# Decode attention of a streaming encoder on one core: the value products as fp32 matmuls on four 32-column tiles, the score products queued together

## The chip, the cores and the metric

The kernel runs as one program on one core of a Trainium2 chip. The metric is the device time of one execution in microseconds (us). Three executions of the kernel before took 1247.17, 1244.36 and 1243.08 us; the median is 1244.36 us. The engines are named as in the profile: PE is the matrix engine (PEld its weight loads), DVE the vector engine, ACT the scalar engine, POOL the gpsimd engine, SP the engine that here only issues DMAs.

## The reference, cut to what matters

One step of an encoder with two layers for two groups of requests: a prompt of 1024 new rows, and 8 running streams ("sequences") of 16 new rows each, whose 1024 old rows of keys and values lie in a cache. Layer 0 holds differential attention with 4 heads beside a gated MLP, and layer 1 a convolution. All is fp32. The change is in the attention of the 8 sequences:

```python
# per sequence: 16 queries, 4 heads, 1024 cached rows and 16 new ones; two maps c = 0, 1 of 64 columns each
s = jnp.einsum('bqhcd,bkhcd->bhcqk', q, k).astype(jnp.float32) * (A_HALF_DIM ** -0.5)
s = s + bias                                   # by relative position
p = jax.nn.softmax(s, axis=-1)
w = p[:, :, 0] - lam * p[:, :, 1]              # differential weights
o = jnp.einsum('bhqk,bkhe->bqhe', w, v)        # values, 128 columns a head
o = _rmsnorm(o, subln_g) * (1.0 - LAMBDA_INIT_0)
out_a = o.reshape(bsz, t, A_WIDTH) * jax.nn.silu(g_a)
y = x + jnp.einsum('bte,ed->btd', jnp.concatenate([out_a, out_b], axis=-1), w_out)
```

## The kernel before

**Stages.** Up to about 480 us the kernel makes the input projection and the attention and MLP of the prompt (its last pieces run beside the start of the next stage). From about 490 to 770 us runs the decode stage, `phase_decode`, which is what the change touches. Behind it stands layer 1 in its convolution form, `phase_conv`, up to the end at 1242 us.

**The decode stage** does two kinds of work at once. One is the attention of the 8 sequences. The other is the output projection of layer 0, `main(t)`, for the nine 128-row tiles t of prompt and sequences: 48 matmuls of 512 columns each in fp32r (L155, tile `out`), with `prep(t)` ahead of it, which loads the tile's inputs (`raw<-s_oa`, `raw<-s_ob`, L829 and L830) and transposes them (L165). The loop at the end of `phase_decode` runs over the sequences b and issues for each: the scores of b, `prep(b-2)`, the keys of b+1 (two of four chunks), the values of b-1, `main(b-2)`, the other two chunks of keys, the weights of b. Pieces of the load and split of `w_out0` (`wl`) lie between them in the first rounds.

- `keys_part` loads a 512 KB chunk of the key cache on SP's queue (L696) into a tile `raw`, of which there are three, shared with the loads of `prep` and `w_out0`; PE transposes it (L416, tile `tr`), and ACT and DVE copy the result into the tile `KT`, or `KTx` for the last chunk, which also holds the new keys (L417).
- `dscores` multiplies keys by queries: for each of four parts of the keys, four matmuls, one a head, on four tiles of 32 columns of the array (L730). A bias, a row maximum (L735) and an exponential (L743) follow.
- `dweights` turns the exponentials into transposed, folded weights `wt` with 9 small matmuls (L758), and splits them into an fp32r high part (ACT, L761) and an fp32r rest (DVE, L762).
- `dvalues` loads four 512 KB chunks of the value cache on POOL's queue into two buffers `vraw` (L772), splits each into `vh` (ACT, L775) and `vl` (DVE, L776), and makes two matmuls of 512 columns in fp32r for each of 9 key tiles (L783, L784, and L786 for the new values `vs`). As every query row meets all four heads' columns, a mask keeps its own head (`om`, L788), an fp32 matmul puts the 16 rows in their place among 128 (L790), and DVE adds them to `oacc` (L794).
- `dfinish` normalises `oacc` once behind the last sequence, multiplies it by the gate and stores it to `s_oa`, from which `prep(8)` reads.

**What sets the order.** The code is handed to a scheduler that places each instruction on its engine by a simulated timeline, so that the order on an engine is not the order of the code. `tc.high_priority(offset=...)` moves what is issued under it ahead in this order. Each engine then runs its list strictly in order, and waits where a value isn't there yet. POOL and SP issue their DMAs from these lists too.

Of the kernel before, what the change touches and what calls it, by code (L numbers as in the profile page):

```python
# [19 lines left out]
P = 128  # L20
# [61 lines left out]
C_W = C_SAME + P  # L82
PE_TILES = (2, 4, 6)
# [19 lines left out]
class Builder:  # L103
# [544 lines left out]
    def decode_begin(self):  # L648
# [8 lines left out]
        vs = [ep.tile([P, 512], F32R, name=f"vs{i}", bufs=1) for i in range(2)]  # L657
        qs = [ep.tile([P, H, P], F32, name=f"qs{i}", bufs=1) for i in range(2)]
        oacc = ep.tile([P, 512], F32, name="oacc", bufs=1)
        mk = ep.tile([P, C_SGN - C_FOLD], F32, name="mk", bufs=1)  # L660
        fold, own, place = mk[:, :64], mk[:, 64:576], mk[:, 576:]
# [3 lines left out]
        def setup():  # L665
            nc.sync.dma_start(out=mk, in_=a["cst"][:, C_FOLD:C_SGN])
# [8 lines left out]
            nc.sync.dma_start(out=raw[:, 512:], in_=self.v0s)  # L675
            self.kt_copy(raw[:, :512], kTs, ptc, nc.scalar.copy)
            nc.scalar.copy(vs[0], raw[:, 512:])
            nc.vector.tensor_tensor(vs[1], raw[:, 512:], vs[0].bitcast(F32), ALU.subtract)
# [27 lines left out]
        self.dec = dec, ep, vp, ptc, vs, oacc, fold, own, place, bs0, seqs, keys_part, qz  # L706
        return [setup] + [lambda i=i: keys_part(0, (i,)) for i in range(4)]

    def phase_decode(self):
        nc, tc, a = self.nc, self.tc, self.a  # L710
        dec, ep, vp, ptc, vs, oacc, fold, own, place, bs0, seqs, keys_part, qz = self.dec
# [4 lines left out]
        pm = E(tc.tile_pool(name="pa", bufs=2, space=PSUM, reuse_waits="tile"))  # L716
# [3 lines left out]
        def dscores(b):  # L720
            q = qz[b % 2]
            S = []
            nm = self.small.tile([P, 4], F32, name="nm3")
            for i, parts in enumerate(((0, 1), (2,), (3,))):
                s = pS.tile([P, 512], F32, name="S")
                for j, p in enumerate(parts):
                    kt = seqs[b]["K"][p]
                    n = kt.shape[2]
                    for h in range(H):
                        nc.tensor.matmul(s[h * 32:(h + 1) * 32, j * n:(j + 1) * n], lhsT=q[:, h, :],  # L730
                                         rhs=kt[:, h, :], start=True, stop=True)
                S.append(s)
# [19 lines left out]
        def dweights(b):  # L752
            ex, cf = seqs[b]["ex"], seqs[b]["cf"]
            wt = ep.tile([P, 9, P], F32R, name="wt", bufs=1)
            for g0, g1 in ((0, 8), (8, 9)):
                ps = pm.tile([P, 512], F32, name="mm")
                for k in range(g0, g1):
                    nc.tensor.matmul(ps[:, (k - g0) * 64:(k - g0 + 1) * 64], lhsT=ex[:, k, :], rhs=cf,  # L758
                                     start=True, stop=True)
                pv = ps[:, :(g1 - g0) * 64].rearrange("p (k e) -> p k e", e=64)  # L760
# [452 lines left out]
```

## Time and profile before

| what | value |
|---|---|
| three executions | 1247.17, 1244.36, 1243.08 us |
| the profiled execution, its own time | 1244.07 us |
| its span in the trace | 1242.3 us |
| granted PE clock, mean | 0.975 of full |
| DVE busy | 807.9 us (65%) |
| ACT busy | 461.0 us (37%) |
| POOL busy | 364.3 us (29%) |

The span is what the trace covers; 1.8 us of the execution's own time lie around it. Times "at 652 us" below are counted from the start of the span. An fp32 matmul has two records in the trace, an fp32r matmul one. A record's duration overlaps the next one, so that what a matmul costs in a dense stretch is read from the distance of one start to the next.

### The profile page before, as it was taken

Reading aid. Unit: us, or ns where it says so; the run is one execution under the profiler, and the core shown is the slowest. Engines: PE = TensorE matmul, PEld = TensorE weight load, DVE = VectorE, ACT = ScalarE, POOL = GpSimd, SP = SyncE. Lnnn points to the kernel's source line nnn. Section 1 sums busy time; section 2 is a strip of 40 time slices with the busy share of each in tenths; the row PEclk is TensorE's granted clock in tenths of the full one; section 3 lists DMA queues with packets and bytes.
Section 4 is the critical chain, followed back from the end, with each engine's and each line's share of the span. In section 5 each row is a group of like instructions: output and inputs, shape, how many; then the busy total and the mean of one; then the engine's idle time right before and its main releaser. Section 6 shows DMA issues by size and latency. Waiting matters only on the chain.

```text
span 1242.3 us, 18215 instructions
## 1 busy us (share of the span) xinstructions
PE 1163.6 (94%) x6516; PEld 1038.4 (84%) x6516; DVE 807.9 (65%) x1663; ACT 461.0 (37%) x1058; POOL 364.3 (29%) x516
## 2 busy tenths in 40 slices
PE   6999999999989997779999998999999987998997
PEld 4878998999989987557776767999999987997886
DVE  5420225688787778765555444899989999267843
ACT  4431223545454545554435334111121212256421
POOL 2232223344354335322322220112424220033300
PEclk9999999999989998889999999999999998999999
DMA  8352444414141314877766646113321310212231
GB/s 298 107 157 73 148 145 136 126 55 120 41 122 46 103 49 137 287 246 238 238 220 237 194 145 174 45 41 89 97 85 60 112 60 24 68 35 102 80 124 68
DMA packets 122042, 153.23 MB, mean 123 GB/s; under 512 B 13697, under 2 KB 85401, under 8 KB 121944
## 3 DMA queue, kind: packets, MB, share of 16 engines
q1 hardware_dynamic: 107968, 108.21, 28.1%
q0 software_dynamic: 13840, 43.60, 10.5%
q8 instruction: 52, 0.85, 0.3%
q14 instruction: 38, 0.31, 0.1%
q10 hardware_dynamic: 144, 0.26, 0.1%
HBM read 116.22 MB, written 36.26 MB: 123 GB/s over the span
## 4 chain that ended last, share of the span: by engine, by line
PE 75%; DMA 9%; DVE 6%; issue 5%; ACT 3%; POOL 1%; SPq 0%; DVEq 0%; POOLq 0%; ACTq 0%
PE mm L155 51%; PE out L155 7%; PE py L1172 3%; PE pa L587 2%; PE tr L416 2%; DMA vraw<-in_cache_v 1%; PE tr L165 1%; PE S L544 1%; PE mm L784 1%; PE S L545 1%; PE mm L783 1%; PE tr L582 1%; DMA big<-s_c 1%; DMA s_c<-big 1%; PE S L730 1%
## 5 line engine op out<-in xcount | busy, mean ns | idle before, releaser
L155 PE MATMUL mm<-yh,wh 128*128 128x384 f32 x576 | 196.4, 341 | 15.2 <-ACT sg L1021 12.7
L155 PE MATMUL mm<-yh,wl 128*128 128x384 f32 x576 | 195.4, 340 | 0.2 <-DVE wl L144 0.2
L155 PE MATMUL mm<-yl,wh 128*128 128x384 f32 x576 | 195.4, 339 | 0.0
L155 PE MATMUL mm<-wh,xh 128*128 128x384 f32 (+1 forms) x504 | 185.4, 369 | 1.5 <-DVE sg L467 0.6
L1148 DVE SCALAR_TENSOR_TENSOR acc<-u,cc,acc 128x1024 f32<-128x1024 f32 x145 | 185.7, 1281 | 0.4
L155 PE MATMUL mm<-wl,xh 128*128 128x384 f32 (+1 forms) x504 | 184.3, 366 | 1.5 <-DVE wl L144 1.5
L155 PE MATMUL mm<-wh,xl 128*128 128x384 f32 (+1 forms) x504 | 183.5, 364 | 0.0
L144 DVE TENSOR_TENSOR wl<-raw,wh 128x1024 fp32r<-128x1024 f32 (+1 forms) x72 | 91.3, 1275 | 91.8 <-ACT wh L143 88.4
L155 PEld LDWEIGHTS mm<-yh,wh 128*128 128x128 f32 x576 | 109.2, 190 | 16.0 <-ACT sg L1021 13.0
L155 PEld LDWEIGHTS mm<-yh,wl 128*128 128x128 f32 x576 | 109.1, 190 | 0.6 <-DVE wl L144 0.5
L155 PEld LDWEIGHTS mm<-yl,wh 128*128 128x128 f32 x576 | 109.2, 190 | 0.3
L155 PEld LDWEIGHTS mm<-wh,xh 128*128 128x128 f32 x504 | 95.7, 190 | 13.1 <-issue 1.1
L155 PEld LDWEIGHTS mm<-wl,xh 128*128 128x128 f32 x504 | 95.6, 190 | 11.4 <-DVE wl L144 2.9
L155 PEld LDWEIGHTS mm<-wh,xl 128*128 128x128 f32 x504 | 95.5, 189 | 8.8 <-DVE xl L168 0.3
L143 ACT CAST wh<-raw 128x1024 fp32r<-128x1024 f32 (+1 forms) x72 | 71.4, 1001 | 70.0 <-PE mm L155 32.2
L124 POOL TENSOR_TENSOR rr<-pw,mhalf 128x1 f32<-128x1 f32 x59 | 38.4, 651 | 165.9 <-DVE pw L123 157.4
L558 ACT ACTIVATE e<-S,nm 128x512 f32<-128x512 f32 (+5 forms) x96 | 55.0, 578 | 53.7 <-DVE nm L553 36.2
L155 PE MATMUL out<-wh,ch 128*128 128x512 f32 x144 | 59.9, 416 | 1.7 <-DVE xr L844 1.2
L1166 POOL TENSOR_TENSOR tw<-wx,same 128x640 f32<-128x640 f32 x24 | 37.3, 1558 | 82.3 <-PE py L1172 72.5
L550 DVE TENSOR_REDUCE nm<-S 128x1 f32<-128x512 f32 (+5 forms) x96 | 52.5, 551 | 10.5 <-PE S L545 9.7
L155 PE MATMUL out<-wh,cl 128*128 128x512 f32 x144 | 58.8, 408 | 0.0
L155 PE MATMUL mm<-wl,ch 128*128 128x512 f32 x144 | 56.4, 392 | 2.3 <-DVE wl L144 2.2
(282 smaller groups left out, 2400.0 us busy)
## 6 DMA issues: line engine op xcount, KB each, us to landing
raw<-in_cache_k SPq DMA_DIRECT2D x32, 512.0 KB, 4.4
vraw<-in_cache_v POOLq DMA_DIRECT2D x32, 512.0 KB, 5.4
raw<-in_w_in SPq DMA_DIRECT2D x24, 512.0 KB, 5.1
raw<-in_w_out SPq DMA_DIRECT2D x16, 512.0 KB, 4.6
raw<-in_w_in SPq DMA_DIRECT2D x32, 256.0 KB, 3.4
raw<-in_w_in SPq DMA_DIRECT2D x48, 128.0 KB, 3.1
s_y<-xr POOLq DMA_DIRECT2D x9, 512.0 KB, 4.7
x<-s_y SPq DMA_DIRECT2D x9, 512.0 KB, 4.2
```

The lines of the kernel that those rows point to most:

```text
L124: m = nc.gpsimd.tensor_tensor(out, v[:, :w], self.mhalf[:, :w], ALU.pow)
L143: nc.scalar.copy(h[:, :ks * n], raw[:, :ks * n])
L144: (low or nc.vector).tensor_tensor(l[:, :ks * n], raw[:, :ks * n], h[:, :ks * n].bitcast(F32), ALU.subtract)
L155: m = self.nc.tensor.matmul(out, lhsT=x, rhs=y, start=(i == 0), stop=(i == n - 1))
L165: nc.tensor.transpose(ps[:, k * P:(k + 1) * P], src[:, kk * P:(kk + 1) * P], self.ident)
L416: nc.tensor.transpose(ps[:, h * P:(h + 1) * P], src[:, h * P:(h + 1) * P], self.ident)
L550: nc.vector.tensor_reduce(nm[:, j:j + 1], s[:, :n], AX.X, ALU.max, negate=True)
L558: nc.scalar.activation(e[:, j * n:(j + 1) * n], S[j][:, :n], AF.Exp, bias=nv, accum_out=zz[:, j:j + 1])
L587: nc.tensor.matmul(po, lhsT=wT[:, k * P:(k + 1) * P], rhs=hd["v"][:, k, :], start=(k == 0), stop=(k == qb))
L1148: tap = nc.vector.scalar_tensor_tensor(cv[:, :T] if k == CONV - 1 else acc, u[:, k:k + T], w1, acc, ALU.mult, ALU.add)
L1166: nc.gpsimd.tensor_tensor(tw.rearrange("p s (c f) -> p s c f", f=8), wx[:, g, :].rearrange("p (s f) -> p s f", f=8).unsqueeze(2).broadcast ...
L1172: nc.tensor.matmul(py, lhsT=tw[:, 4 - s, :], rhs=X[:, g, s:s + 176], start=(s == 0), stop=(s == 4))
```

## The change

The values stay fp32 and are not split. For each of the 9 key tiles, four matmuls of 128 columns, one a head, with the 16 query columns of that head's weights, write to four tiles of 32 columns of one PSUM bank, `pvt`. So each head's result lies apart: the mask, the placing matmul, `oacc` and `dfinish` go, and with them the split of the values and of the weights. Each sequence's result is squared and summed (ACT), scaled and gated by itself (DVE), with a gate `gs` that is loaded once at the start; the results of sequences 0 to 6 are stored by four DMAs, those of the last by four more. The values' load becomes `vload`, with eight buffers instead of two; the scores' 16 matmuls and the values' 36 are issued under `high_priority`. The scores' parts are taken in the order 3, 2, 0, 1, and the pool `pa` has one bank instead of two.

```diff
+HPS = 300
+VB = 8
...
-        oacc = ep.tile([P, 512], F32, name="oacc", bufs=1)
-        mk = ep.tile([P, C_SGN - C_FOLD], F32, name="mk", bufs=1)
+        fold = ep.tile([P, 64], F32, name="mk", bufs=1)
+        gs = ep.tile([P, NB, P], F32, name="gs", bufs=1)
+        og = ep.tile([P, NB, P], F32, name="og", bufs=1)
...
+            nc.gpsimd.memset(gs, 0.0)
+            for h in range(H):
+                nc.sync.dma_start(out=gs[h * 32:h * 32 + NQ], in_=self.s_ga[T:, h * P:(h + 1) * P].rearrange(
+                    "(b q) e -> q b e", q=NQ))
+            nc.sync.dma_start(out=vs, in_=self.v0s)
...
-            for i, parts in enumerate(((0, 1), (2,), (3,))):
+            S = [pS.tile([P, 512], F32, name="S") for _ in range(3)]
+            with tc.high_priority(offset=HPS):
+                for p, i, j in ((3, 2, 0), (2, 1, 0), (0, 0, 0), (1, 0, 1)):
...
+            wt = ep.tile([P, 9, 64], F32, name="wt", bufs=2)
...
+            nc.scalar.copy(wt[:, :8], ps.rearrange("p (k e) -> p k e", e=64))
+            nc.vector.tensor_copy(wt[:, 8], p8)
...
+        def vload(b):
+            if b >= NB:
+                return
+            cv = a["cache_v0"][b].rearrange("(t p) h e -> p t (h e)", p=P)
+            seqs[b]["V"] = []
+            for i in range(4):
+                vr = vp.tile([P, 1024], F32, name="vraw", bufs=VB).rearrange("p (t c) -> p t c", t=2)
+                nc.gpsimd.dma_start(out=vr, in_=cv[:, 2 * i:2 * i + 2])
+                seqs[b]["V"] += [vr[:, 0], vr[:, 1]]
+            seqs[b]["V"].append(vs)
...
         def dvalues(b):
-                    nc.scalar.copy(vh, vr)
-                    (nc.vector if i in VDVE else nc.gpsimd).tensor_tensor(vl, vr, vh.bitcast(F32), ALU.subtract)
...
-            nc.vector.tensor_tensor(om, pav, own, ALU.mult)
-            po = pm.tile([P, 512], F32, name="mm")
-            nc.tensor.matmul(po, lhsT=place[:, 112 - NQ * b:240 - NQ * b], rhs=om, start=True, stop=True)
...
+            pav = pvt[:, b % 2 * P:(b % 2 + 1) * P]
+            with tc.high_priority(offset=HPS):
+                for k in range(8, -1, -1):
+                    for h in range(H):
+                        nc.tensor.matmul(pav[h * 32:h * 32 + NQ], lhsT=wt[:, k, h * NQ:(h + 1) * NQ],
+                                         rhs=V[k][:, h * P:(h + 1) * P], start=(k == 8), stop=(k == 0))
...
+            nc.scalar.activation(jk, pav, AF.Square, accum_out=ss)
+            rm = self.small.tile([P, 1], F32, name="rr")
+            self.rpow(rm, ss, 1.0 / P, 1e-6)
+            nc.vector.scalar_tensor_tensor(og[:, b], pav, rm, gs[:, b], ALU.mult, ALU.mult)
...
         for b in range(NB):
             dscores(b)
...
             if b > 0:
                 dvalues(b - 1)
+                vload(b)
...
-        dfinish()
```

Three places show what the scheduler makes of it. The first is PE's list in a steady round, around the scores of a middle sequence (its queries are `qz_5777`; `tr` are transposes, of the keys under L416 and of `prep`'s input under L165). Before, word for word:

```order
L416 MATMUL tr<-cst_58,raw 128x128 x8
L758 MATMUL mm<-cf,ex 128x64 x9
L730 MATMUL S<-KT,qz_5777 32x256 x3
L416 MATMUL tr<-cst_58,raw 128x128 x4
L730 MATMUL S<-KT,qz_5777 32x256 x5
L165 MATMUL tr<-cst_58,raw 128x128 x4
L783 MATMUL mm<-vh,wt 128x512
L784 MATMUL mm<-vl,wt 64x512
```

Four pairs of value products (L783, L784) stand there in all, and then the last part of the scores, on `KTx`. In the changed kernel the same engine has, at the same place of a round (L736 are the scores, L786 the values, L418 and L167 the two kinds of transposes, L157 the output projection):

```order
L786 MATMUL pv<-vs,wt 16x128 x4
L786 MATMUL pv<-vraw,wt 16x128 x32
L157 MATMUL out<-wl,ch 128x512
L157 MATMUL out<-wh,cl 128x512
L157 MATMUL out<-wh,ch 128x512
L157 MATMUL out<-wl,ch 128x512
L157 MATMUL out<-wh,cl 128x512
L418 MATMUL tr<-cst_58,raw 128x128 x12
L167 MATMUL tr<-cst_58,raw 128x128 x4
L736 MATMUL S<-KTx,qz_5777 32x272 x4
L736 MATMUL S<-KT,qz_5777 32x256 x12
L167 MATMUL tr<-cst_58,raw 128x128 x4
```

The scores, which stood in three to four pieces between transposes and value products, are one piece of 16, and the values one of 36; the scores begin with the last chunk's part, right behind its transposes. Behind these rows stand 11 matmuls of the output projection before the next chunk of keys is transposed.

The second place is ACT's list between the last key copies of one round and the exponentials that follow (L743 before, L748 now). Before:

```order
L417 COPY KT<-tr 128x4x128
L173 ACTIVATE yn,ss<-xr 128x1024
L775 CAST vh<-vraw 128x1024
L177 ACTIVATE yn<-xr,rr 128x1024
L775 CAST vh<-vraw 128x1024
L417 COPY KTx<-tr 128x4x128
L167 CAST ch<-tr 128x512 x2
```

And now (L175 is the sum of squares over a finished tile of the output projection, L790 that over a sequence's values, L419 the key copies):

```order
L175 ACTIVATE yn,ss<-xr 128x1024
L419 COPY KT<-tr 128x4x128
L790 ACTIVATE jk,ss<-pv 128x128
L419 COPY KTx<-tr 128x4x128
L169 CAST ch<-tr 128x512
L179 ACTIVATE yn<-xr,rr 128x1024
L169 CAST ch<-tr 128x512
```

The casts of values are gone, a small sum of squares came in, and the copy into `KTx` stands behind both sums.

The third place is POOL's list where the decode stage starts (L772 and L776 load chunks of the value cache; L483, L469 and L485, L471 are MLP work of the prompt). Before:

```order
L738 MEMSET ex 128x128
L690 MEMSET qz_5778 128x128
L772 DMA vraw<-in_cache_v 128x2x512 x2
L483 TENSOR_TENSOR z_5513<-z_5510,lnb 128x128
L483 TENSOR_TENSOR z_5588<-z_5585,lnb 128x128
L469 TENSOR_TENSOR hh<-gl,sg 128x128
L772 DMA vraw<-in_cache_v 128x2x512
```

And now:

```order
L669 MEMSET gs 128x1024
L694 MEMSET qz_5777 128x128
L776 DMA vraw<-in_cache_v 128x2x512 x4
L743 MEMSET ex 128x128
L694 MEMSET qz_5778 128x128
L776 DMA vraw<-in_cache_v 128x2x512 x4
L485 TENSOR_TENSOR z_5513<-z_5510,lnb 128x128
```

Eight chunks, those of sequences 0 and 1, are issued where two were, ahead of the same MLP work, and a memset of the gate's tile stands in front.

81 lines of the change are left out of this document (22 added, 59 removed).

## The prediction

> **What bounds the kernel now.** I read the page first: the busy shares, the slices and the chain of work that ended last.
>
> ```profile
> span 1242.3 us, 18215 instructions
> PE 1163.6 (94%) x6516; PEld 1038.4 (84%) x6516; DVE 807.9 (65%) x1663; ACT 461.0 (37%) x1058; POOL 364.3 (29%) x516
> PE   6999999999989997779999998999999987998997
> PE 75%; DMA 9%; DVE 6%; issue 5%; ACT 3%; POOL 1%; SPq 0%; DVEq 0%; POOLq 0%; ACTq 0%
> ```
>
> PE is busy for 94% and carries 75% of the chain. The slices have one dip before the end, the 777 of the 16th to 18th slice, which is 466 to 559 us: the start of the decode stage. So the windows of that stage come next, cut at the start and then by rounds (PE's busy time is the second number, then the other engines, the granted clock, the DMA share and the rate):
>
> ```profile
> core 0: us, PE busy (x) PEld busy (x) DVE busy (x) ACT busy (x) POOL busy (x), PEclk, DMA share, GB/s
> 490.00:510.00 20.00, 14.07 (x95) 12.29 (x94) 16.30 (x48) 12.10 (x33) 9.00 (x20) 0.83 0.91 282
> 510.00:530.00 20.00, 11.23 (x107) 7.39 (x105) 11.04 (x24) 8.37 (x18) 4.57 (x10) 0.83 0.80 276
> 530.00:550.00 20.00, 16.27 (x98) 10.74 (x98) 15.61 (x23) 13.09 (x25) 4.68 (x6) 0.83 0.73 254
> 577.00:604.00 27.00, 27.00 (x165) 20.21 (x165) 15.77 (x29) 13.44 (x27) 11.20 (x13) 1.00 0.80 261
> 657.50:684.00 26.50, 26.03 (x159) 19.00 (x158) 15.32 (x26) 11.95 (x23) 6.99 (x10) 1.00 0.71 239
> 684.00:711.00 27.00, 24.45 (x118) 18.64 (x117) 13.87 (x22) 10.84 (x22) 5.81 (x8) 0.94 0.58 191
> ```
>
> The stage has two halves. From 490 to 550 PE idles for 5.9, 8.8 and 3.7 us, while the DMA share is 0.73 to 0.91. From 577 on a round takes 26.5 to 27 us and PE is full; ACT and DVE work about half of it. **What leaves PE in these rounds shortens them; what leaves DVE and ACT does not.** The chain of waits at the start says what the first half waits for:
>
> ```profile
> 504.68 4.76 DMA raw<-in_cache_k
> 516.81 6.55 DMA raw<-in_w_out
> 525.72 3.54 DMA raw<-in_w_out
> 544.02 6.51 DMA raw<-s_ob
> ```
>
> Loads of keys, of `w_out0` and of the first tile's inputs end the waits there.
>
> **The change part by part.** The rows of one round on PE:
>
> ```profile
> 651.40 1.03 PE L416 MATMUL tr<-cst,raw 128*128 128x128 f32 x8
> 652.36 0.64 PE L730 MATMUL S<-KT,qz 128*32 128x256 f32 x8
> 652.93 0.51 PE L783 MATMUL mm<-vh,wt 128*128 128x512 f32 x1
> 653.27 0.39 PE L784 MATMUL mm<-vl,wt 128*64 128x512 f32 x1
> 653.51 0.39 PE L783 MATMUL mm<-vh,wt 128*128 128x512 f32 x1
> ...
> 594.99 0.86 PE mm L790 x2
> ...
> 512.25 1.50 PE L730 MATMUL S<-KT,qz 128*32 128x256 f32 x24
> 513.57 0.64 PE L730 MATMUL S<-KTx,qz 128*32 128x272 f32 x8
> ```
>
> *Values (1).* Before, from start to start, a value product costs 0.24 us (653.27 to 653.51; I use 0.23 as the mean of such pairs), and a sequence has 18, so 4.1, and the placing matmul takes 0.86: 4.95 to 5.0 us. Afterwards there are 9 groups of four matmuls, 72 records. No row shows a 128-column matmul on a 32-column tile. The nearest is the scores: 24 records start within 1.32 us (512.25 to 513.57), so 0.055 a record and 0.44 for a group of 8 at 256 columns. One full-width record of 512 columns takes 0.43 (half of 0.86), so a record of 256 columns alone would take 0.215, and eight in 0.44 are four side by side with nothing left over. At 128 columns the group lies between 0.22, half of that, and 0.44, if a record costs 0.055 whatever its width. I take 0.30, nearer the lower end, since the scores' row shows no fixed cost above its streaming. Nine groups are 2.7; entering and leaving the tiled stretch I put at 0.3, of which more below. So 3.0 instead of 4.95 for each of six sequences (2 to 7): −1.95 × 6 = −11.7. The values of sequence 1 were multiplied beside the first full round; in the new order they stand ahead of the first output tile, where PE idles, so there the whole 4.95 leaves the full half. Sequence 0 was in the idle half before and stays. **Together −16.65.**
>
> The Trainium skill, page "TensorEngine Tiling (Array Packing)", section Instruction Overhead, speaks against taking so small a tile: each matmul has some 60 cycles of overhead on trn2, and the tiling factor should not be taken from a dimension that is already small. If that came on top of the streaming of 128 columns, a group would be near the upper bound and not at 0.30, and the time 1236.6 instead of 1229, which is the first rival below; the scores' row of this case shows no such addition at 256 columns, and no row shows 128.
>
> *Scores (2).* A group of eight records in a piece of its own takes 0.57 (652.36 to 652.93) instead of 0.44, and the rows beside such a piece stretch: 652.93 to 653.27 is 0.34 instead of 0.23. So a piece costs about 0.13 and some 0.1 to 0.2 beside it, 0.3 in all; this is also where the 0.3 of (1) is from. Three to four pieces become one: −0.75 us in each of five rounds (3 to 7). **−3.75.** That the values become one piece too is counted in (1).
>
> *Waits that go (3).*
>
> ```profile
> PE mm L784 <- DVE vl L776: 0.7, 3, 0.2
> 694.38 1.90 PE L758 MATMUL mm<-cf,ex 128*128 128x64 f32 x16
> 698.51 0.43 PE L758 MATMUL mm<-cf,ex 128*128 128x64 f32 x2 [2.24 <-DVE oacc L794]
> ```
>
> Value products waited 0.7 us in all for the rest `vl`, and the last weights 2.24 us for the bank that `oacc` freed late; behind this the clock in the window 684 to 711 is 0.94 instead of 1.00, 27 × 0.06 = 1.6 us of PE work. Neither `vl` nor `oacc` is left: **−4.** What is late next there is the exponentials of the last sequence, which no row shows to be late. The casts and subtractions of the values (ACT and DVE) go too, but those engines were not full: nothing.
>
> *Weights of sequence 2 (4).* They stood behind the first output tile, and stand ahead of it now, in the idle half. Nine of them cost 18 records at 0.117 (16 in 1.90): **−2.1.** The split of the weights goes, and stood beside other work: nothing.
>
> *Scores that wait for ACT (5), added.* The scores now begin with `KTx`, whose last copy stands on ACT behind two sums of squares.
>
> ```profile
> L844 DVE TENSOR_TENSOR xr<-xr,out 128x512 f32<-128x512 f32 x18 | 12.3, 683 | 29.4 <-PE out L155 29.4
> L173 ACT ACTIVATE yn<-xr 128x1024 f32<-128x1024 f32 x9 | 9.5, 1060 | 8.2 <-DVE xr L844 7.3 <-issue 0.9
> L800 ACT ACTIVATE jk<-oacc x4: 293/310/310, 723.7 to 725.9; 128x128 f32<-128x128 f32 x4
> L417 ACT COPY KTx<-tr x8: 565/577/585, 504.6 to 683.6; 128x512 f32<-128x512 f32 x8
> ```
>
> From the last output product on: DVE adds (0.68), ACT squares the tile (1.06, and 0.2 to read its sum out), squares the sequence's values (0.31, and 0.2), copies `KTx` (0.58): 3.0 us. PE meanwhile has 12 + 4 transposes, at 0.12 each (eight in 0.96, from 651.40 to 652.36): 1.9. So it waits 1.1, and I put 1.2 with the hand-over. Below, nothing, if the copy gets ready by chance; above 1.7, with one more copy (0.58) ahead. Behind the scores on PE's list stand the second half of the input transposes and the next output tile, which has no slack. 1.2 × 5: **+6.** If the scores' wait lasts, the clock may drop too, as it did behind the wait of 2.24.
>
> *The value loads as bursts (6), added.* Four chunks are issued at a time (2 MB) instead of one by one.
>
> ```profile
> 652.03 3.88 SPq L696 DMA_DIRECT2D raw<-in_cache_k  x2
> 660.89 0.60 PE L416 MATMUL tr<-cst,raw 128*128 128x128 f32 x4
> raw<-in_cache_k SPq DMA_DIRECT2D x32, 512.0 KB, 4.4
> vraw<-in_cache_v POOLq DMA_DIRECT2D x32, 512.0 KB, 5.4
> ```
>
> A chunk of keys was issued at 652.03 as its buffer came free, and first used at 660.89: 8.9 us for a landing of 4.4. In the new order its buffer comes free four transposes into the twelve; up to its first use stand 8 + 4 transposes (1.4), the scores (1.8), 4 transposes (0.5) and 11 products (2.5): 6.2 us. At 282 GB/s, the highest rate of the windows, 2 MB take 7.4 us. If both queues share the rate, a chunk that lands in 4.4 alone takes up to twice that, 8.8, whenever it falls into a burst: 2.6 late at most, 15.6 over six bursts. The burst is issued behind the values of the round before, so it falls beside the critical chunk in part only. I take 0.6 a burst, +3.5, with bounds of 0 and 15.6.
>
> *The start (7), added.* The 2 MB of sequence 1 are issued with those of sequence 0, at a DMA share of 0.91, and four loads of the gate, and `vs`, stand on SP's queue ahead of the queries and keys.
>
> ```profile
> 485.82 4.27 DMA gah<-s_ga
> 490.12 4.74 DMA qs<-s_ql
> ```
>
> The queries stand on the chain at 490, so a delay there counts. Bound above: the full 7.4 us of the 2 MB. Below: −3, since of PE's idle 8.8 us a part waited for splits that go. The nearest fact is that the window's rate was already the highest, and that PE idles through it: a part of the 7.4 is bytes that must come in any case by 550. I take **+2**.
>
> POOL gets the memset of the gate and one power more per sequence, SP eight small stores: POOL is at 7 of 26.5 us a round, so nothing. The stores of sequence 7 lead to the last tile's input, which is behind two other tiles: nothing, and about 3 us (their landing) if that cover is gone.
>
> The sum: −16.65 − 3.75 − 4 − 2.1 + 6 + 3.5 + 2 = −15.0 us. The profiled execution took 1244.07, with 1.8 us around its span, and is 0.3 below the median of the three: 1244.07 − 15.0 = **1229 us**.
>
> **The rivals.**
>
> *The tiles are bound by issue.* A group costs 0.44. For it: 0.055 is the smallest distance between two records in the trace. Against it: the same row is explained by streaming alone. (0.44 − 0.30) × 9 = 1.26 a sequence, × 6 = 7.6: 1236.6. Chance 0.15.
>
> *The start is late by the whole burst.* 7.4 instead of 2: 1234.5. For it the DMA share of 0.91; against it that the loads of `w_out0`, which end the waits, are issued later than V1. Chance 0.10.
>
> *Keys land behind the values' burst (slower).* Place: the first chunk of keys of each round. If SP's chunk stands behind the whole 2 MB, it lands after 7.4 + 4.4 = 11.8, with a cover of 6.2: 5.6 × 6 = 34 instead of 3.5: 1259. It turns the gain into a loss from (15 + 3.5) / 6 = 3.1 us a round. For it: the cover shrinks from 8.9 to 6.2, and POOL's chunk already takes 5.4. Against it: two queues, and a landing of 4.4 in windows at 0.71 to 0.80. Chance 0.10.
>
> The Trainium skill, page "DMA: Bandwidth & Descriptors", section SWDGE vs HWDGE vs iDMA, has the two kinds of queues feed different queues inside each DMA engine, which goes round between them. By that rule keys would share with values and not stand behind them, which speaks for at most 15.6 (1241) and against 34 (1259); no row of this case shows a burst of four chunks beside keys.
>
> *The change doesn't do what it says: the 16-column tiles run one behind the other.* An untiled fp32 record of 128 columns:
>
> ```profile
> 220.71 1.78 PE pa L587 x16
> ```
>
> 0.111 × 72 = 8.0, with 0.3: 8.3 instead of 3.0, × 6 = 32: 1261. Against it stands the scores' row, four tiles side by side. Chance 0.05.
>
> **How the numbers follow.** The forecast has 0.60. Its own spread, with the bounds of (1), (5), (6) and (7) partly adding up, is 1214 to 1243: below, tiles at 0.22 (−4.3) and no wait for ACT (−6) and no late keys (−3.5); above, the start late by 7.4 and 1.5 a burst. The first two rivals lie inside. The last two, 0.15, lie above and stay out; 1214 to 1246 leaves them and a little more of the edges. A measurement of this kernel tells about 0.3% from no change, 3.7 us: faster is below 1240.6, slower above 1248.1. Faster: nine tenths of the forecast, 0.54, and most of the first two rivals, 0.20: 0.74. Same: the rest of these, 0.11. Slower: the last two rivals, 0.15.
>
> **What would show it.** (1) a sequence's 36 value products as one piece of 2.7 us at 0.30 a group, 4.0 at 0.44, 8.0 if they run one behind the other. (2) 16 scores in 1.8 to 1.9 us. (3) no wait of the weights for DVE. (5) scores on `KTx` with 1.2 us idle ahead, released by ACT. (6) transposes of keys released by the keys' DMA, below 1 us a round. (7) the first output tile begins no more than 2 us later relative to the queries. Rounds of 24 to 25 us instead of 26.5. The forecast is wrong if rounds stay at 26.5 while the values got shorter: then a wait has taken the place of the work.

## The result, and the profile after

The changed kernel took 1254.22 us (median of five, 1251.48 to 1258.58) beside 1245.0 for the kernel before (median of five): a ratio of 1.008, with a 95% interval of 1.0051 to 1.0109. It is slower, where 1229 and a range of 1214 to 1246 were forecast. The profiled execution took 1254.22 us with a span of 1252.4, 10.1 more than before. First the page of the changed kernel: span, PE, its slices and clock, and the chain.

```profile
span 1252.4 us, 18924 instructions
...
PE 1147.3 (92%) x6932; PEld 1036.9 (83%) x6932; DVE 756.2 (60%) x1618; ACT 429.9 (34%) x1025; POOL 359.5 (29%) x523
...
PE   6999999999989997479989998999989987999997
...
PEclk9999999999989999789999998999999997999999
...
PE 76%; DMA 10%; DVE 5%; ACT 3%; issue 3%; POOL 2%; SPq 0%; DVEq 0%; POOLq 0%; ACTq 0%
```

PE's work did get less, 1163.6 to 1147.3 us, and DVE and ACT lost more. But PE is busy for a smaller share of a longer span: waits took the place of the work. Where they are is read from two marks on PE: the first output product (tile `out`), and the first product of layer 1 (`mm<-yh,wh`), each in the group rows of its tile, which give the first and the last start. Before, and then after:

```profile
L155 PE MATMUL out<-wh,ch x144: 387/392/799, 551.1 to 754.2; 128*128 128x512 f32 x144
...
L155 PE MATMUL mm<-yh,wh x576: 332/334/689, 755.7 to 1127.8; 128*128 128x384 f32 x192
```

```profile
L157 PE MATMUL out<-wh,ch x144: 387/393/774, 566.2 to 754.8; 128*128 128x512 f32 x144
...
L157 PE MATMUL mm<-yh,wh x576: 331/334/687, 755.6 to 1136.8; 128*128 128x384 f32 x192
```

The first output tile begins 15.1 us late. Layer 1 nevertheless begins when it did, so the decode stage's gains had just made up for its start. And then layer 1, whose code is the same, takes 1252.4 − 755.6 = 496.8 us instead of 486.6. **In this execution the whole loss appears in a part of the kernel that was not changed.** The windows show the waits of the decode stage; first the one from 631 us of the kernel before, then the start and two rounds after (their columns are those of the prediction's windows):

```profile
631.00:657.50 26.50, 26.25 (x160) 19.06 (x158) 15.69 (x26) 12.21 (x25) 8.12 (x13) 1.00 0.71 242
```

```profile
490.00:510.00 20.00, 9.34 (x60) 8.09 (x60) 11.38 (x36) 6.52 (x20) 6.83 (x16) 0.77 0.97 313
510.00:530.00 20.00, 11.66 (x94) 8.32 (x93) 10.38 (x26) 8.27 (x18) 7.56 (x15) 0.89 0.79 255
...
604.00:631.00 27.00, 24.34 (x278) 19.61 (x280) 7.72 (x19) 8.10 (x20) 8.96 (x14) 1.00 0.67 235
631.00:657.50 26.50, 21.16 (x150) 16.72 (x139) 8.40 (x20) 8.21 (x20) 7.72 (x13) 0.94 0.70 239
```

From 490 to 510 PE is busy for 9.34 us instead of 14.07 at a DMA share of 0.97; and in the window from 631, where it worked 26.25 of 26.5 us, it now idles for 5.3. The chain of waits at the start, and then the timeline of the changed kernel from 629 us on, with the rows of PE, POOL and SP that matter:

```profile
488.34 7.60 DMA gs<-s_ga
495.96 9.61 DMA qs<-s_ql
```

```profile
629.20 0.41 PE L786 MATMUL pv<-vs,wt 128*16 128x128 f32 x8
...
629.43 1.93 PE L786 MATMUL pv<-vraw,wt 128*16 128x128 f32 x64
630.38 2.90 POOL L776 DMA_DIRECT2D vraw<-in_cache_v  x4 [5.37 <-PE pv L786]
631.29 0.50 PE L157 MATMUL out<-wh,cl 128*128 128x512 f32 x1
...
633.39 5.95 SPq L700 DMA_DIRECT2D raw<-in_cache_k  x3
...
636.39 0.67 PE L736 MATMUL S<-KTx,qz 128*32 128x272 f32 x8 [0.33 <-ACT KTx L419]
...
636.85 1.50 PE L736 MATMUL S<-KT,qz 128*32 128x256 f32 x24
...
643.46 0.63 PE L418 MATMUL tr<-cst,raw 128*128 128x128 f32 x4 [4.06 <-DMA raw<-in_cache_k]
```

The value products free four buffers at once, POOL issues the 2 MB, and right behind them the first chunk of keys gets its buffer. It lands by the time its transposes start, 10 us after its issue, and PE stands idle for 4.06 of them. The queues show why. In the first 4 us from the chunk's issue (633.39 to 637.39) only `software_dynamic` moved packets, the queue of POOL's DMAs: the values, and a 512 KB store `s_y` that POOL issued behind them. In the next 4 us the keys' queue, `hardware_dynamic`, moved 0.44 MB beside it:

```profile
q0 software_dynamic: 338, 1.21, 91.9%
```

```profile
q0 software_dynamic: 267, 0.99, 71.5%
q1 hardware_dynamic: 216, 0.44, 28.7%
```

The queries, which landed in 4.74 us before, take 9.61, and were issued 6 us later too.

### The profile page after: what moved, and what is told of

It is laid out like the page before. It is cut to its first block, busy times and chain, and to the rows that moved or that the text cites. A ratio compares the mean times of both kernels' runs of the same rounds, so it can differ in the third digit from the quotient of the medians.

```text
span 1252.4 us, 18924 instructions
## 1 busy us (share of the span) xinstructions
PE 1147.3 (92%) x6932; PEld 1036.9 (83%) x6932; DVE 756.2 (60%) x1618; ACT 429.9 (34%) x1025; POOL 359.5 (29%) x523
## 3 DMA queue, kind: packets, MB, share of 16 engines
q0 software_dynamic: 13760, 43.33, 10.1%
## 4 chain that ended last, share of the span: by engine, by line
PE 76%; DMA 10%; DVE 5%; ACT 3%; issue 3%; POOL 2%; SPq 0%; DVEq 0%; POOLq 0%; ACTq 0%
PE mm L157 53%; PE out L157 8%; PE py L1162 3%; DMA raw<-in_cache_k 3%; PE pa L589 2%; PE tr L167 1%; DMA raw<-in_w_in 1%; PE pv L786 1%; PE S L546 1%; PE tr L418 1%; PE S L547 1%; PE mm L763 1%; PE tr L584 1%; DVE wl L146 1%; DMA qs<-s_ql 1%
## 5 line engine op out<-in xcount | busy, mean ns | idle before, releaser
L157 PE MATMUL mm<-yh,wh 128*128 128x384 f32 x576 | 198.4, 344 | 15.1 <-ACT sg L1011 12.6
L157 PE MATMUL mm<-yl,wh 128*128 128x384 f32 x576 | 197.3, 342 | 0.0
L157 PE MATMUL mm<-yh,wl 128*128 128x384 f32 x576 | 196.7, 342 | 0.0
L157 PE MATMUL mm<-wh,xh 128*128 128x384 f32 (+1 forms) x504 | 185.2, 369 | 1.3 <-DVE sg L469 0.6
L157 PE MATMUL mm<-wl,xh 128*128 128x384 f32 (+1 forms) x504 | 184.2, 366 | 1.7 <-DVE wl L146 1.7
L157 PE MATMUL mm<-wh,xl 128*128 128x384 f32 (+1 forms) x504 | 183.3, 364 | 0.0
L157 PEld LDWEIGHTS mm<-yh,wh 128*128 128x128 f32 x576 | 110.4, 192 | 15.9 <-ACT sg L1011 12.8
L157 PEld LDWEIGHTS mm<-yl,wh 128*128 128x128 f32 x576 | 110.8, 192 | 0.3
L157 PEld LDWEIGHTS mm<-yh,wl 128*128 128x128 f32 x576 | 110.7, 192 | 0.1
L157 PEld LDWEIGHTS mm<-wh,xh 128*128 128x128 f32 x504 | 95.5, 190 | 12.7 <-issue 1.1
L157 PEld LDWEIGHTS mm<-wl,xh 128*128 128x128 f32 x504 | 95.6, 190 | 11.8 <-DVE wl L146 3.2
L157 PEld LDWEIGHTS mm<-wh,xl 128*128 128x128 f32 x504 | 95.4, 189 | 8.9 <-DVE xl L170 0.3
L157 PE MATMUL out<-wh,ch 128*128 128x512 f32 x144 | 59.5, 413 | 2.5 <-DVE xr L833 2.1
L418 PE MATMUL tr<-cst,raw 128*128 128x128 f32 x260 | 38.7, 284 | 24.7 <-DMA raw<-in_cache_k 16.5
L157 PE MATMUL out<-wh,cl 128*128 128x512 f32 x144 | 59.2, 411 | 0.0
L157 PE MATMUL mm<-wl,ch 128*128 128x512 f32 x144 | 56.9, 395 | 2.3 <-DVE wl L146 2.2
```

The costliest lines, as they stand in the source:

```text
L157: m = self.nc.tensor.matmul(out, lhsT=x, rhs=y, start=(i == 0), stop=(i == n - 1))
L418: nc.tensor.transpose(ps[:, h * P:(h + 1) * P], src[:, h * P:(h + 1) * P], self.ident)
```

## The experiments

Each ran beside the kernel before. Ratios are to it, with their 95% intervals. "Layer 1" is from its first product to the end of the span, in the profiled execution.

### The changed kernel again, and two parts of its start

No edit:

> The changed kernel once more, for a second profile. From its first product of layer 1 (755.6 us) to the end of the span it took 496.8 us, the kernel before 486.6. If this loss belongs to the kernel (its order in layer 1), it is 494 to 499 us again. If it is chance of one execution, it lies anywhere from 486 to 499, and the first scores still start near 522 us and rounds still take 23 to 29 us.

1254.04 us, ratio 1.0070 (1.0048 to 1.0093). First scores at 522.5, layer 1 493.6 us. The loss in layer 1 is there again, though 3 us smaller. It lies just below the 494 to 499 that were expected if it belongs to the kernel, so this run alone doesn't tell the two cases apart.

```diff
-VB = 8
+VB = 4
```

> Four value buffers instead of eight: the values of sequence 1 are loaded only behind the value products of sequence 0. Theory 1 (the 4 MB of values ahead of the queries make the start late): the first scores start at 513 to 516 us instead of 521.8, and the time falls by 4 to 8 us. Rival (the four gate loads ahead of the queries on SP make it late): the start stays at 520 to 522, and the time within 2 us. Theory 2 (keys late behind a burst of values issued just before them) is left untouched: rounds of 25 to 29 us with waits for the keys' DMA stay.

1254.52 us, ratio 1.0072 (1.0047 to 1.0097). The first scores start at 512.75, as theory 1 has it, and the first output product at 557.2 instead of 566.2. But layer 1 begins at 753.8, 1.8 us earlier only. The rounds got longer, 27.2 us instead of 25.6 (from the scores of sequence 3 to those of 7, by four), and between 550 and 700 us the transposes of keys wait 10.2 us for their DMA, where they waited 7.1 in the changed kernel. Of the 15.1 us at the start 9.0 go with four of the eight value buffers, and the time does not fall by the 4 to 8 us that were expected, since the rounds behind wait for keys.

```diff
-            nc.gpsimd.memset(gs, 0.0)
-            for h in range(H):
-                nc.sync.dma_start(out=gs[h * 32:h * 32 + NQ], in_=...)
...
             dscores(b)
+            if b == 1:
+                nc.gpsimd.memset(gs, 0.0)
+                for h in range(H):
+                    nc.sync.dma_start(out=gs[h * 32:h * 32 + NQ], in_=...)
```

> The gate's memset and its four loads are issued behind the scores of sequence 1 in the code, so that the queries and the first keys go ahead of them on SP. Theory 1 (value bursts): queries still land near 504 us, the first scores at 519 to 522 us, time within 2 us. Rival (gate loads): queries land at 496 to 499 us, first scores at 514 to 517 us, time 4 to 7 us lower.

1257.48 us, ratio 1.0105 (1.0052 to 1.0157); first scores at 520.3. The chain shows why:

```profile
487.43 13.73 DMA qs<-s_ql
```

The queries are issued 8.5 us earlier and land at 501.2 instead of 505.6, between the two expectations: beside the 4 MB of values they now take 13.73 us. The first scores gain only 1.5 us, where half the values in e2 gained 9.1. So it is the values in the main, not the gate's small loads.

### Buffers of their own for the keys

`kraw` takes the keys' chunks out of the three buffers that they shared with `prep` and `w_out0`. In e4 and f1 it has four buffers; in f4 three, beside the eight of the values. e4 keeps e2's four value buffers.

```diff
-                kr = self.rawp.tile([P, 1024], F32, name="raw").rearrange(...)
+                kr = vp.tile([P, 1024], F32, name="kraw", bufs=4).rearrange(...)
```

> As e2_vb4, with four buffers for the keys alone instead of three shared with the other loads, so that a chunk of keys is issued a whole round ahead of its use. Theory 2 (keys late behind values): no wait of the key transposes for the keys' DMA in the rounds, rounds of 22.5 to 24 us, and 5 to 8 us below e2_vb4. Rival (the rounds are long for the waits on ACT for KTx and for the transposes' banks): rounds stay at 24 to 26 and the time within 2 us of e2_vb4. Layer 1 as in e1_again.

> The kernel before, with four buffers for the keys alone. In the changed kernel (with four value buffers) this took the start of layer 1 from 753.8 to 728.3 us. Theory A (the change is worth its 20 us and more once the keys come early; before it, the keys were not late): the kernel before gains at most 5 us, 1240 to 1247. Rival (the buffers are worth the 25 us by themselves, whatever the values are): 1218 to 1226, start of layer 1 at 730 to 735 us.

> The changed kernel with its eight value buffers, and three buffers for the keys alone. Theory 2 (keys late behind a burst of values, as their buffer came free only then): rounds of 23 to 23.5 us without a wait for the keys' DMA, as in e4_kraw4, though the bursts are as long as before. Rival (it was the eight value buffers together with the burst, and four are needed): waits for keys of 2 to 4 us in some rounds, 25 us and more. At the start the 4 MB of values stand ahead of the queries again: first scores at 520 to 523 us, and the time 2 to 8 us above e4_kraw4.

| values' / keys' buffers | start of layer 1 | rounds from sequence 3 to 7 | median | ratio |
|---|---|---|---|---|
| before, keys shared | 755.7 | 26.5 | 1245.0 | 1 |
| f1: before, keys own 4 | 749.7 | 27.1 | 1240.20 | 0.9956 (0.9938 to 0.9973) |
| after: 8, shared | 755.6 | 25.6 | 1254.22 | 1.0080 (1.0051 to 1.0109) |
| e2: 4, shared | 753.8 | 27.2 | 1254.52 | 1.0072 (1.0047 to 1.0097) |
| f4: 8, own 3 | 739.7 | 23.0 | 1239.43 | 0.9946 (0.9925 to 0.9966) |
| e4: 4, own 4 | 728.3 | 23.0 | 1229.78 | 0.9871 (0.9826 to 0.9916) |

A round is a quarter of the time between the scores of sequences 3 and 7. These two rows are, in the changed kernel and then in e4:

```profile
588.00 0.67 PE L736 MATMUL S<-KTx,qz 128*32 128x272 f32 x8 [1.01 <-ACT KTx L419]
...
690.23 0.67 PE L736 MATMUL S<-KTx,qz 128*32 128x272 f32 x8 [1.01 <-ACT KTx L419]
```

```profile
571.77 0.67 PE L736 MATMUL S<-KTx,qz 128*32 128x272 f32 x8 [0.92 <-ACT KTx L419]
...
663.79 0.67 PE L736 MATMUL S<-KTx,qz 128*32 128x272 f32 x8 [0.67 <-ACT KTx L419]
```

With own buffers the rounds of the changed kernel take 23.0 us each, in f4 as in e4, though a burst is as long as ever; so theory 2 holds, with the shared buffer as the cause and the eight value buffers without blame for the rounds. The gain was underrated: e4 lies 24.7 us below e2, where 5 to 8 were expected. In f4 the first scores start at 526.6, later than the 520 to 523 expected, and the first output product at 566.4, so the eight buffers do cost the start: 739.7 − 728.3 = 11.4 us (the fourth key buffer is in this difference too). The kernel before gains 6.0 us up to layer 1 by the same buffers, so the rival of f1 falls. With them in both, the change brings layer 1 forward by 749.7 − 728.3 = **21.4 us**; the medians of f1 and e4 lie 10.4 us apart, as e4's layer 1 takes 497.3 us and f1's 487.3. What f1 gains it gains at the start, not in its rounds. The first output tile of f1, and then of e4:

```profile
L155 PE MATMUL out<-wh,ch x144: 387/389/793, 544.8 to 749.0; 128*128 128x512 f32 x144
```

```profile
L157 PE MATMUL out<-wh,ch x144: 387/393/504, 551.1 to 726.8; 128*128 128x512 f32 x144
```

So beside a kernel with the same key buffers the start of e4 is still 6.3 us late. Two rounds of e4 show what is left in the rounds:

```profile
594.00:617.00 23.00, 22.09 (x211) 17.99 (x210) 8.41 (x21) 8.08 (x22) 8.34 (x13) 1.00 0.76 277
617.00:640.00 23.00, 22.09 (x212) 18.00 (x210) 8.41 (x21) 8.08 (x22) 8.33 (x13) 1.00 0.78 276
```

PE idles for 0.9 us in a round.

### Layer 1

In layer 1 data go to memory and back several times between groups of products (stores `s_c<-big` and `s_u<-big`, and loads back), and these round trips stand on the chain. In the kernel before the first two stores of `s_c` took 3.7 us, in the changed one 5.1 and 5.2. The DMA view, cut from the second store's issue on, with its 40 slices of 0.15 us in GB/s; the kernel before (from 959.9 us) and the changed one (from 964.4):

```profile
GB/s 0 0 0 0 0 0 145 319 319 324 324 310 324 314 324 305 329 314 329 310 324 188 5 0 0 0 0 0 0 0 0 263 263 75 113 263 188 413 225 338
...
s_c<-big SPq DMA_DIRECT2D x1, 704.0 KB, 3.7
```

```profile
GB/s 0 0 0 0 109 0 61 305 296 310 310 286 296 310 319 291 286 314 329 314 319 249 47 19 19 23 23 23 19 19 19 0 0 0 0 0 0 0 0 0
...
q8 instruction: 1, 0.02, 1.4%
...
s_c<-big SPq DMA_DIRECT2D x1, 704.0 KB, 5.2
```

The store runs as fast in both, and then has a tail of 1.3 us at some 20 GB/s; a packet of 0.02 MB on the queue `q8 instruction` went out just ahead of it (the 109). The tail at a sixteenth of the rate is read as one of the 16 DMA engines that had the instructions first and ends last; no view shows the engines one by one. The Trainium skill (page "Runtime: NRT & Kernel Launch", section Instruction fetch mechanics) has each engine's instructions come in blocks of 16 KiB, 256 instructions, and calls the cost of crossing from one to the next mostly hidden. The trace agrees with the size: the profile of the kernel before lists 52 such packets with 0.85 MB, 16 KB each, and PE's 13,032 records are about 51 times 256. Behind 700 us they stand 252 PE records apart on average, whether that takes 20 or 36 us, so they are read as PE's. What shows here is a cost in another place than PE, at the store beside the load. If these are PE's, their place hangs on PE's count of instructions, which the change had moved. The test adds tiny fp32 matmuls ahead of PE's first one, whose result nobody reads; each has two records for the product and two for its weights, four instructions. The edit, with 19 in f2, 25 in f3 and g4, 40 in h1, 64 in h2:

```diff
+            with tc.tile_pool(name="pad", bufs=1, space=PSUM, reuse_waits="tile") as padp:
+                pad = padp.tile([P, 512], F32, name="pad")
+                for _ in range(19):
+                    nc.tensor.matmul(pad[:16, :1], lhsT=self.mhalf, rhs=self.mhalf[:, :1], start=True, stop=True)
```

> The kernel before, with 19 tiny fp32 matmuls (76 instructions) on PE ahead of its first one, where PE idles. In layer 1 of the changed kernels the stores of s_c that had a load of PE's instructions beside them took 4.8 to 5.3 us, the others 3.7; in the kernel before these loads fall 4 to 7 us behind the stores. Theory B (the place of the instruction loads costs layer 1 its time, and it hangs on PE's count of instructions): with 76 more they fall into the stores, s_c takes 4.9 to 5.3 us twice, layer 1 takes 490 to 494 us instead of 486.6, and the time rises by 3 to 7 us. Rival (the order of layer 1 in the changed kernel costs it): s_c stays at 3.7, layer 1 at 486 to 487, the time within 2 us.

> e4_kraw4 with 25 such matmuls (100 instructions) ahead. Theory B: the loads of PE's instructions move some 9 us ahead, out of both stores of s_c; these take 3.7 us, layer 1 takes 490 to 494 us instead of 497.3 (its start, 2.9 us late by its order, stays), and the time falls by 3 to 7 us below e4_kraw4. Rival: layer 1 at 496 to 498, time within 2 us of e4_kraw4.

> The changed kernel itself with 25 tiny matmuls (100 instructions) ahead on PE and nothing else. Theory B (instruction loads beside the stores of s_c): both stores back at 3.7 us, layer 1 at 489 to 492 us instead of 496.8, time 3 to 7 us below the changed kernel (1247 to 1251). Its decode stage is as before: start of layer 1 at 755 to 758 us. Rival (layer 1 is slow for its order): layer 1 at 494 to 498, time 1252 to 1256.

> The changed kernel with 40 tiny matmuls (160 PE instructions) ahead. In g4 (100) the profile had layer 1 at 487.5 us, but of six executions three took 1246 to 1250 and three 1255 to 1258. With 160 the instruction loads should lie some 14 us ahead of their places in the changed kernel, farther from every store and load of s_c and s_u. Theory B: layer 1 at 487 to 491 us, the median 1246 to 1251, few executions above 1253. Rival (something else in layer 1 costs the changed kernel 7 us, and g4's profile was a lucky execution): the median stays at 1252 to 1256.

> The control: 64 tiny matmuls are 256 PE instructions, which is about one load of instructions (0.85 MB in 52 loads are 16 KB, 256 instructions of 64 bytes), so the loads fall on the same places of layer 1 as in the changed kernel. Theory B: both stores of s_c at 4.8 to 5.3 us again, layer 1 at 493 to 497, time 1252 to 1257. Rival (the tiny matmuls help by themselves, as by a warmer clock at the start): layer 1 at 487 to 491, time 1245 to 1250.

| kernel | instructions added | first two stores of s_c | layer 1 | median | ratio |
|---|---|---|---|---|---|
| before | 0 | 3.7, 3.7 | 486.6 | 1245.0 | 1 |
| f2: before | 76 | 4.6, 5.1 | 493.4 | 1251.46 | 1.0053 (1.0032 to 1.0074) |
| e4 | 0 | 4.8, 5.0 | 497.3 | 1229.78 | 0.9871 (0.9826 to 0.9916) |
| f3: e4 | 100 | 3.7, 3.7 | 490.9 | 1223.80 | 0.9832 (0.9793 to 0.9871) |
| after | 0 | 5.1, 5.2 | 496.8 | 1254.22 | 1.0080 (1.0051 to 1.0109) |
| g4: after | 100 | 3.7, 3.7 | 487.5 | 1252.42 | 1.0070 (1.0036 to 1.0104) |
| h1: after | 160 | 3.7, 3.7 | 486.8 | 1251.20 | 1.0041 (1.0017 to 1.0065) |
| h2: after | 256 | 5.1, 5.4 | 494.4 | 1258.58 | 1.0100 (1.0068 to 1.0132) |

As to the stores every profile falls as theory B says, f2's first one 0.3 us below its range: the loads can be moved into the stores of the kernel before, out of those of e4 and the changed kernel, and a whole period of 256 leaves them where they were. The profiles of all 17 kernels agree. The 20 first and second stores with a load beside them took 4.2 to 6.0 us, the 14 others 3.7. From the first store to the end of the span it took 350.0 to 353.3 us in the seven kernels whose stores were free, and 354.2 to 361.4 in the other ten. Ahead of the first store layer 1 takes 135.3 to 141.0 us, and that part doesn't follow the stores: g3 (below) has both at 3.7 and still a layer 1 of 494.3, for its first store is issued 141.0 us after the start. Some of that may be loads beside other transfers (a load back from `s_u` took 6.4 us there), which wasn't tested. The slow store in h2 (cut from 967.6 us) has the same tail and the same packet:

```profile
GB/s 0 0 0 109 0 23 263 305 314 296 286 310 305 296 291 324 314 300 300 329 286 75 19 19 19 19 23 23 19 19 19 9 0 0 0 0 0 0 0 0
...
q8 instruction: 1, 0.02, 1.7%
```

The times follow in part. The medians of g4 (1252.42, expected 1247 to 1251) and h1 (1251.20, expected 1246 to 1251 with few executions above 1253, where four of twelve are) miss theory B's range, g4's into that of its rival. f2 and h2 are clear of their neighbours: f2 is above its kernel by an interval clear of 1, and the intervals of h2 and h1 don't meet; of the 10.9 us between their profiled spans (1255.9 and 1245.0) 7.6 lie in layer 1 and 3.3 ahead of it. Between e4 and f3 the medians differ by 6.0, but their intervals overlap. g4's six executions took 1246.48 to 1257.73, three below 1250 and three above 1255, and h1's twelve spread evenly over 1246.25 to 1256.42, where the profiled ones (1246.99 and 1246.87) are among the shortest; the kernel before itself spread from 1241.29 to 1253.13 beside h1. So in the changed kernel itself moving the loads makes the short executions possible, but does not hold them; what lengthens the others isn't shown, since they have no profile.

### Pieces, priority, and the best version

```diff
-HPS = 300
+HPS = 0
```

> e4_kraw4 with the priority offset at 0: the scheduler now places a sequence's values in four rows (4 and 15, 5, 12 matmuls, with transposes between) and leaves the scores in one. Theory (an extra piece costs some 0.3 us for entering and leaving the tiled stretch): two more pieces are 0.6 us a round, rounds of 23.5 to 23.7 instead of 23.0, time 2 to 5 us above e4_kraw4. Rival (the pieces cost nothing, or stand in the waits that are there): rounds at 23.0, time within 2 us.

The rounds went to **22.08** us, not 23.5 to 23.7 (four rounds from 570.33 to 658.65). The values stand in three pieces between the last transposes. PE's rows there, first e4 and then g1:

```profile
638.92 0.65 PE L418 MATMUL tr<-cst,kraw 128*128 128x128 f32 x4 [0.24 <-ACT KT L419]
...
640.79 0.67 PE L736 MATMUL S<-KTx,qz 128*32 128x272 f32 x8 [0.67 <-POOL rr L126]
```

```profile
612.14 0.66 PE L418 MATMUL tr<-cst,kraw 128*128 128x128 f32 x4
612.72 0.61 PE L786 MATMUL pv<-vraw,wt 128*16 128x128 f32 x10
613.26 0.66 PE L167 MATMUL tr<-cst,raw 128*128 128x128 f32 x4
613.85 0.85 PE L786 MATMUL pv<-vraw,wt 128*16 128x128 f32 x24
614.52 0.64 PE L736 MATMUL S<-KTx,qz 128*32 128x272 f32 x8
```

The pieces fill the two waits of 0.24 and 0.67 us, and cost less than they fill. The time, 1223.64 us (0.9833, 0.9803 to 0.9863), carries a layer 1 of 500.3 us with instructions beside both stores (5.2 and 5.8).

```diff
-                for p, i, j in ((3, 2, 0), (2, 1, 0), (0, 0, 0), (1, 0, 1)):
+                for p, i, j in ((0, 0, 0), (1, 0, 1), (2, 1, 0), (3, 2, 0)):
```

> e4_kraw4 with the scores' parts in the order 0, 1, 2, 3: with the priority the scheduler places each part as soon as its keys are there, so the scores fall into four pieces, and KTx comes last. Theory of the prediction (0.3 us for a piece, and some 0.7 to 0.9 us a round of waiting for the copy into KTx): three more pieces cost 0.9, the wait goes: rounds of 23.0 to 23.3 and the time within 3 us of e4_kraw4. Rival (the wait for KTx costs and the pieces don't): rounds of 22.2 to 22.4, time 3 to 5 us lower.

1227.05 us (0.9856, 0.9833 to 0.9879); rounds of 22.7, between the two theories: the scores in four pieces, so a little is gained by the wait that goes, and the pieces cost less than 0.9.

g3 puts e4, the late gate and 100 instructions together; h3 is the same with the priority offset at 0.

> f3_kraw4_pad (four buffers for the keys alone, four for the values, 100 PE instructions ahead) with the gate's loads behind the queries and first keys. The queries are issued near 487 instead of 495 us. Theory 1 (the loads of the start stand one behind the other, so what goes ahead comes early): first scores at 507 to 511 us instead of 514.4, first output tile at 543 to 548 instead of 550.5, time 2 to 7 us below f3_kraw4_pad (1217 to 1222). Rival (the first output tile waits for the weights and the tile's inputs, not for the scores): out at 550 or later, time within 2 us of f3_kraw4_pad.

> Four buffers for the keys alone, four for the values, the priority offset at 0 as in g1, the gate's loads behind the queries, and 100 PE instructions ahead. g1 had rounds of 22.1 us (23.0 with the priority) but layer 1 at 500.3, with instruction loads in both stores of s_c. If the two add up: rounds of 22.1, layer 1 at 490 to 495, time 1213 to 1220. If the shorter rounds only move other waits, or the loads fall into other transfers of layer 1: 1220 to 1226.

g3: 1221.80 us (0.9814, 0.9783 to 0.9846), first scores at 516.2 and the first output product at 551.4, so its rival holds, and the gate's place is worth nothing. h3: **1213.97 us, ratio 0.9734 (0.9698 to 0.9770)**, rounds of 22.1 and layer 1 at 490.8: the two gains add up, and the version beats both kernels.

## Why the prediction was wrong

The forecast had layer 1 begin 15 us earlier, at 740.7, and not change. It began at 755.6, and took 10.2 longer. By the steps of the prediction:

**Values (1): right in kind, too dear.** 3.0 us a sequence were taken; the 72 records stand within 2.09, 0.029 a record, and some 0.2 go beside them: 2.3. That is 0.23 a group, near the streaming bound of 0.22; six sequences gain 4 us more than forecast. The first rival (0.44 a group) falls, and the fourth (untiled) too. The first leaned on 0.055 as the smallest distance of two records, and that was a mean: in the trace before, the four records of the scores' quartet start 6 to 7 ns apart, and the next quartet 0.2 us later. The values' quartets stand 0.110 us apart. The Trainium skill (page "TensorEngine Tiling (Array Packing)", section Instruction Overhead) has some 60 cycles of overhead for each matmul; at 128 columns on four tiles this trace shows none on top of the streaming.

**Scores (2): the price of a piece was wrong.** 0.3 us a piece were taken from a row of transposes and products around it. g1 has two more pieces and is faster by 0.92 us a round. Queueing the values whole, which (1) and (2) counted as a gain, costs a little: pieces can fill waits.

**Waits (3) and ACT (5).** No weights wait for `oacc`, and the longest wait of theirs for DVE is 0.6 us. The scores waited 3.4 us in all for ACT's copy of `KTx`, where 6 were taken: the mechanism was right, the size within its bounds.

**Bursts (6): the right mechanism and place, mis-sized.** The cover was 6 us, as was worked out; but the chunk took 10 us (by sharing, 8.8 was the most). 0.6 was taken because the burst should fall beside the critical chunk in part only. It was issued from 630.38 on, wholly ahead of the chunk (633.39). The rounds of the changed kernel average 25.6 us, those of e4 23.0: 2.56 a round, at the upper bound of 2.6, where 0.6 was taken. Over the four rounds that is 10.2, of which 7.1 are seen as waits for keys, against the 3.5 counted. The third rival (stand behind the whole burst, 5.6 a round) was too much; that its 1259 lies near the measured 1254 is chance, since it wanted 34 us from the bursts. The Trainium skill (page "DMA: Bandwidth & Descriptors", section SWDGE vs HWDGE vs iDMA) has each DMA engine go round between the queues of the two kinds. The trace agrees in part: for 4 us behind its issue the keys' queue moved nothing, and in the next 4 us it had 0.44 MB beside 0.99.

**The start (7): the step that failed most.** +2 us were taken, and the first output tile began 15.1 us late, beyond the upper bound of 7.4. The bound counted the bytes of sequence 1 once. But these 2 MB and those of sequence 0 went out within 6 us, ahead of the queries; these were issued later, landed in 9.6 instead of 4.7 us, and keys and `w_out0` came behind them. With four value buffers it begins at 557.2 (e2), and with own key buffers too at 551.1 (e4), as before; beside f1, which has the same key buffers, 6.3 us of lateness stay. The argument that "PE idles through it" was turned round: the idle time was what the loads already cost.

The four terms together, an account by the trace and not a test: +13.1 (start), +6.7 (bursts), −2.6 (ACT), −4.2 (values) give 13.0 of the 14.9 us by which the decode stage missed its forecast.

**Layer 1: no step at all.** The prediction did not ask what the same code behind the change would do. In the profiled execution its 10.2 us are read as follows: 2.9 ahead of the first products with `py` (none in e1), 1.4 and 1.5 in the two stores of `s_c`, 2.1 between the second store and the end of the last `py`, and 2.3 spread over the rest. So the two stores themselves are 2.9 of it. By PE's own account the 10.2 are 6.3 us more busy time for the same products, at a lower granted clock, and 3.9 us more idle time. Layer 1 as one window, before and after:

```profile
755.70:1242.30 486.60, 456.21 (x2511) 432.23 (x2510) 375.07 (x579) 136.48 (x294) 112.48 (x100) 0.98 0.25 79
```

```profile
755.60:1252.40 496.80, 462.53 (x2507) 438.75 (x2505) 373.89 (x578) 135.54 (x292) 109.83 (x100) 0.97 0.24 77
```

A lower clock behind a longer wait is seen at one place: in the window from 976 us PE idles for 2.59 us instead of 0.55, and behind that the granted clock is 0.51 for 3.4 us. The rows from 976 us after and before, and between them the one from 992.4 us after:

```profile
976.00:996.00 20.00, 17.41 (x93) 17.04 (x93) 18.48 (x24) 4.14 (x9) 5.85 (x5) 0.91 0.42 131
...
992.40:995.80 3.40, 3.40 (x13) 3.40 (x12) 3.40 (x7) 0.31 (x1) 1.55 (x1) 0.51 0.02 5
```

```profile
976.00:996.00 20.00, 19.45 (x116) 19.11 (x115) 20.00 (x31) 2.01 (x6) 4.74 (x5) 1.00 0.39 127
```

f2 shows that the loads' place alone lengthens layer 1 of the kernel before by 6.8 us, of which 2.3 are in its two stores. By which path the rest follows from them (the clock, other waits) is argued, not shown.

## What to carry to other kernels

Freed compute time is only worth something where the loads have room for it: ask for each buffer that a load waits for who frees it, and what else is issued at that moment, and for the first loads of a stage what stands ahead of them in bytes. When a change alters how many instructions an engine has, look at the DMA round trips on the critical chain behind it, even in code that is the same. And a row of instructions without gaps isn't better than one in pieces, if a piece fills a wait.

## What the runs showed of the hardware that was not expected

A 704 KB store that runs at some 300 GB/s ends in 3.7 us, or in 4.6 to 5.4 (kernels after, f2, e4, h2; 4.2 to 6.0 over all kernels) if one 16 KB load of PE's instructions goes out beside it, where that load is 2% of the bytes. Where it falls moved with the number of PE instructions far ahead: 76, 100 and 160 more moved it, 256 more brought it back. And four fp32 matmuls of 128 columns, each on its own tile with 16 columns in use, ran at 0.029 us a record, 0.110 for the four, where one on the whole array takes 0.111. Last, keys that were issued 3 us behind a burst of 2 MB on another queue moved no packet for 4 us.
